# Norm factors as rows: from matrix products to a trip through device memory, with the first norm's sums taken by one column of ones

## The chip, the core and the metric

The kernel runs on one core of one Trainium2 chip. The metric is the device time of one execution in microseconds (us), as the median of several runs. TensorE is called PE below, VectorE DVE, ScalarE ACT, GpSimd POOL; SP is the engine that issues most of the DMAs, and it issues them in a fixed order.

## What is computed

One encoder layer on x (1024 positions x 1024 features, float32). Only the two norms at which the change acts are shown; attention and the delta rule lie between them.

```python
def rms_norm(x, g):
    y = x * rsqrt(mean(x * x, axis=-1) + EPS)
    return y * g

u = rms_norm(h, mix_norm_gain);  proj = u @ w_in      # 3592 columns: q, k, v, delta q, k, v, gate, decay, beta
...                                                   # band attention and gated delta rule give `mixed`
h = h + mixed
z = rms_norm(h, ffn_norm_gain) @ w_ff1                # 1024 -> 4096
h = h + square(relu(z)) @ w_ff2                       # 4096 -> 1024
```

The kernel multiplies without the norm's factor r = rsqrt(mean + EPS) of each position and applies r to the product. For the second norm the factor enters after the squared relu, as r squared, which is 1 / (mean + EPS).

## The kernel before

Activations lie transposed: features on the 128 partitions, positions along the row. A position's factor is thus needed in two forms: as a **row** (the same 512 or 1024 factors on each of the 128 partitions), to multiply a product whose positions run along the row, and as a **column** `r_col` (128 x 8, position on the partition), for products that stand the other way.

Every product of the large weights is made of three passes over high and low parts (`mm3`, line 217; `uh`/`ul` are the parts of the activations, `wdk_h`/`wdk_l` and so on those of the weights). 24 products of 128 x 128 by 128 x 512 fill one PSUM bank.

**First stage.** `load_xt` (line 232) loads the input in two halves of 512 positions (`hf` 0 and 1), splits it, and adds the squares of the features into two accumulators per half (`xs`; one is added to by DVE, the other by POOL). `first_proj` (line 354) makes the delta k projection: half 0 in four banks (three of pool `ps_a`, one of `ps_o`), half 1 in three (two of `ps_d`, one of `ps_t`). Its fourth tile is made later by `delta_proj` in a bank of `ps_a`. `row_scales` (line 304) is called once per half. It has eight products of an accumulator's 128 columns as stationary operand with one column of ones, which leave the sums as a column (`rcol`); `rsqrt` (line 184) with short instructions on DVE, one of them on POOL (`pow`), which gives `r_col`; and four products of the broadcast column with the identity, which leave the row in PSUM (`rrow`), from where ACT copies it to `rr`. `delta_proj` (line 365) then empties each bank on DVE with `raw = ps * rr` (line 378), convolves (lines 382 and 384) and writes `kT`. The same loop serves delta q (`dq`) and v (`dv`): eight tiles of 24 products each, whose banks are the three of `ps_a` in turn (`dk` half 0 tiles 0 to 2, the fourth tile of half 1, then `dq` 0, 1, 2 and so on). So `dq` tile 2 takes the bank of the fourth `dk` tile of half 1.

**Second norm, in `ff1`** (line 1259). The squares' sums over the features, gathered as `sq_dr`, come back as `acc`; `norm_col` (line 1297) makes eight column products (`hcol`) and a reciprocal on DVE (`r_col`); `norm_row` (line 1308) makes eight products with the identity (`hrow`), and ACT scales them by 1024 into `r2` (128 x 1024). `emit` (line 1355) multiplies each 128 x 1024 block `z` by `r2` on DVE (line 1356) and stores it. Blocks 0 and 1 begin before the norm is known: their first two products `z11` are held, and are multiplied by `r2` once it is there. The weights of `ff1` come by SP (line 1320), and DVE and ACT make high and low parts and sums of weights and activations for PE (lines 204, 1290, 1376, 1395).

The order of the instructions on each engine is made when the program is built: a scheduler replays the code with its own costs and sets the order on every engine, SP included. In the attention part a `Clock` with hand-made costs sets the order.

Of the kernel before, what the change touches and what calls it, by code (L numbers as in the profile page):

```python
# [98 lines left out]
def hymba_kernel(  # L99
# [53 lines left out]
    def bank(pool, name):  # L153
        return pool.tile([P, 512], F32, tag="bk", name=name)
# [29 lines left out]
    def rsqrt(st, ss, n, scale, eps, name, out=None):  # L184
        eng = nc.vector if st in RS else nc.gpsimd
        v = small(st, name + "_v", n)
        eng.tensor_scalar(v, ss, scale, eps, ALU.mult, ALU.add)
        y = small(st, name + "_y", n)
        nc.gpsimd.tensor_tensor(y, v, mhalf[:, 0:n], ALU.pow)
        t = small(st, name + "_t", n)  # L190
        r = small(st, name + "_r", n) if out is None else out
        eng.tensor_tensor(t, y, y, ALU.mult)
        if st in RS:
            nc.vector.scalar_tensor_tensor(t, t, -0.5, v, ALU.mult, ALU.mult)
            nc.vector.scalar_tensor_tensor(r, t, 1.5, y, ALU.add, ALU.mult)
            return r
        nc.gpsimd.tensor_tensor(t, t, v, ALU.mult)
        nc.gpsimd.tensor_scalar(t, t, -0.5, 1.5, ALU.mult, ALU.add)
        nc.gpsimd.tensor_tensor(r, y, t, ALU.mult)
        return r  # L200
# [96 lines left out]
    kt_dr = dram.tile([NT, P, 512], F32, name="kt_dr")  # L297
    h_dr = dram.tile([2, 2, P, 4, TH], F32, name="h_dr")
    f_dr = dram.tile([DFF // P, P, SEQ], F32, name="f_dr")
    sq_dr = dram.tile([P, SEQ], F32, name="sq_dr")  # L300

    mix = [[None, None], [None, None]]

    def row_scales(squares, hf, name, col, row):

        ps = bank(ps_t, f"{name}col{hf}")
        for q in range(TPH):
            for i, acc in enumerate(squares):
                nc.tensor.matmul(ps[:, q:q + 1], acc[:, q * P:(q + 1) * P], ones[:, 0:1], start=(i == 0),
                                 stop=(i == len(squares) - 1))  # L310
        rsqrt("a", ps[:, 0:TPH], TPH, 1.0 / DM, EPS, f"{name}{hf}", col)
        ps = bank(ps_t, f"{name}row{hf}")
        for q in range(TPH):
            nc.tensor.matmul(ps[:, q * P:(q + 1) * P], col[:, q:q + 1].broadcast_to([P, P]), ident,
                             start=True, stop=True)
        nc.scalar.copy(row, ps)

    def interleave(*gens):

# [939 lines left out]
    def ff1(R, started, psw, pools):  # L1259
# [37 lines left out]
        def norm_col():  # L1297

            acc = page2("ut4", "acc")
            nc.sync.dma_start(out=acc, in_=sq_dr)  # L1300
            ps = psw.tile([P, 1024], F32, tag="bk", name="hcol")
            nc.tensor.matmul(ps[:, 0:NT], ones, epsc, start=True, stop=False)
            for q in range(NT):
                nc.tensor.matmul(ps[:, q:q + 1], acc[:, q * P:(q + 1) * P], ones[:, 0:1], start=False, stop=q == NT - 1)
            with tc.issue_after(held[-1][2]), tc.high_priority():
                nc.vector.reciprocal(r_col, ps[:, 0:NT])

        def norm_row():

            ps = psw.tile([P, 1024], F32, tag="bk", name="hrow")  # L1310
            for q in range(NT):
                nc.tensor.matmul(ps[:, q * P:(q + 1) * P], r_col[:, q:q + 1].broadcast_to([P, P]), ident,
                                 start=True, stop=True)
            nc.scalar.mul(r2.rearrange("p a t -> p (a t)"), ps, float(DM))

        def block(sb):
            def lw(tag, name, kh, c):
# [89 lines left out]
        for i in range(2):  # L1407
            for g in first:
                next(g)
        norm_col()  # L1410
        for _ in range(2):
            next(first[0])
        norm_row()
        for emit, z, _ in held:
            emit(z, 0, 0)
        for g in first + [block(sb) for sb in range(2, DFF // FB)]:
# [259 lines left out]
```

## Time and profile before

| | |
|---|---|
| runs | 1263.95, 1261.29, 1260.56 us; median 1261.29 |
| span of the profiled execution | 1256.3 us, first to last instruction (its own device time is not recorded apart from it) |
| granted TensorE clock, mean | 0.998 |
| busy: PE / PE weight loads / DVE / ACT / POOL | 98% / 82% / 74% / 44% / 22% |
| DMA | 158.52 MB in 134374 packets, 126 GB/s on the mean |
| instructions | 17942 |

The busy time of PE is the time between the starts and modelled ends of matmuls that overlap, so 98% says that PE hardly ever stands without work. One fp32 product leaves two records on PE, one product of split (fp32r) operands leaves one. In rows of the timeline the columns are start, duration, engine, line, operation, `out<-in`, shapes and count, and in brackets the idle time before it and what ended it.

### The profile page before, as it was taken

How to read it: one execution, taken by the hardware profiler on the slowest of the kernel's cores; microseconds unless marked ns; L12 is line 12 of the kernel's file. 1: busy time of each engine (PE TensorE's matmuls, PEld its weight loads, DVE VectorE, ACT ScalarE, POOL GpSimd, SP SyncE). 2: the span in 40 equal slices, each digit the busy share in tenths (PEclk: the TensorE clock that was granted, in tenths of full speed). 3: DMA queues.
4: the chain of work that ended last, by engine and by line, in shares of the span. 5: the costliest groups of instructions: out<-in, count | busy, mean ns of one | idle time of the engine just before them, and what ended most of it. 6: DMA issues, size and time to landing. Idle time of an engine off the chain costs nothing.

```text
span 1256.3 us, 17942 instructions
## 1 busy us (share of the span) xinstructions
PE 1236.3 (98%) x6686; PEld 1032.1 (82%) x6686; DVE 932.9 (74%) x1417; ACT 548.1 (44%) x899; POOL 270.5 (22%) x458
## 2 busy tenths in 40 slices
PE   9999999999999999899999999999999999999997
PEld 8778888788889988778888788888887888888886
DVE  7899987755237568776269766767769997997988
ACT  7233132232246756655365444454444543333330
POOL 4425552253133444523200000000000000000043
PEclk9999999999999999999999999999999999999999
DMA  7214364665585633045243333333269614333002
GB/s 228 63 41 141 101 164 118 119 161 134 168 259 136 189 85 88 24 135 176 76 143 104 114 118 118 119 132 101 84 205 365 202 67 134 105 97 101 1 34 100
DMA packets 134374, 158.52 MB, mean 126 GB/s; under 512 B 31120, under 2 KB 78224, under 8 KB 133776
## 3 DMA queue, kind: packets, MB, share of 16 engines
q1 hardware_dynamic: 116192, 135.11, 35.6%
q10 hardware_dynamic: 18096, 22.29, 5.2%
q8 instruction: 52, 0.85, 0.3%
q14 instruction: 34, 0.28, 0.1%
HBM read 109.91 MB, written 47.45 MB: 125 GB/s over the span
## 4 chain that ended last, share of the span: by engine, by line
PE 55%; DVE 5%; ACT 1%; issue 1%; POOL 0%; DVEq 0%; ACTq 0%
PE p L1444 24%; PE q L1348 21%; PE op L222 7%; PE t_o L1026 1%; DVE h L1290 1%; PE t_sa L927 0%; DVE q_0a_l L204 0%; PE t_tpb L987 0%; PE t_tpa L1003 0%; PE t_sb L927 0%; PE c_pv L516 0%; ACT t_pb L966 0%; PE c_po L516 0%; PE t_tpo L520 0%; PE c_pq L516 0%
## 5 line engine op out<-in xcount | busy, mean ns | idle before, releaser
L1516 POOL TENSOR_TENSOR y<-y,y 128x1024 f32<-128x1024 f32 x4 | 11.5, 2890 | 575.7 <-DVE y L1512 570.6
L1512 DVE TENSOR_TENSOR y<-y,p 128x1024 f32<-128x1024 f32 x46 | 55.1, 1217 | 5.4 <-PE p L1444 4.5
L222 PE MATMUL op<-ml,wo_h 128*128 128x512 f32 x128 | 50.2, 395 | 0.0
L222 PE MATMUL op<-mh,wo_h 128*128 128x512 f32 x128 | 49.2, 394 | 0.8 <-ACT mh L203 0.8
L222 PE MATMUL op<-mh,wo_l 128*128 128x512 f32 x128 | 49.3, 391 | 0.0
L947 DVE CUSTOM_DVE_ANT_0 t_pb<-t_sb,biasn 128x256 f32<-128x256 f32 (+1 forms) x64 | 23.2, 401 | 31.4 <-PE t_sb L927 31.3
L966 ACT ACTIVATE t_pb<-t_pb,t_nm 128x256 f32<-128x256 f32 (+1 forms) x64 | 31.4, 491 | 17.2 <-DVE t_nm L958 15.5
L1229 DVE TENSOR_TENSOR h<-op,op_x 128x512 f32<-128x512 f32 x16 | 10.8, 686 | 29.2 <-PE op L222 29.2
L1236 POOL TENSOR_TENSOR op_q<-op_q 128x512 f32<-128x512 f32 x14 | 19.6, 1400 | 55.4 <-ACT op_q L1235 55.1
L222 PEld LDWEIGHTS op<-mh,wo_h 128*128 128x128 f32 x128 | 23.9, 188 | 6.4 <-ACT mh L203 1.2
L222 PEld LDWEIGHTS op<-ml,wo_h 128*128 128x128 f32 x128 | 24.1, 188 | 5.0 <-DVE ml L204 0.2
L222 PEld LDWEIGHTS op<-mh,wo_l 128*128 128x128 f32 x128 | 24.1, 188 | 5.0
L958 DVE CUSTOM_DVE_ANT_0 t_pa<-t_sa,biaso,t_nm 128x384 f32<-128x384 f32 (+2 forms) x48 | 24.9, 543 | 2.8 <-PE t_sa L927 1.6
L970 ACT ACTIVATE t_pa<-t_pa,t_nm 128x384 f32<-128x384 f32 (+2 forms) x48 | 26.5, 552 | 0.0
L222 PE MATMUL aq_ps<-waq_h,ul 128*128 128x512 f32 x64 | 25.5, 399 | 0.0
L222 PE MATMUL dq_ps<-uh,wdq_h 128*128 128x512 f32 x64 | 25.5, 399 | 0.0
L222 PE MATMUL dv_ps<-ul,wdv_h 128*128 128x512 f32 x64 | 25.5, 399 | 0.0
L222 PE MATMUL dq_ps<-ul,wdq_h 128*128 128x512 f32 x64 | 25.3, 396 | 0.0
L222 PE MATMUL g_ps<-ul,wg_h 128*128 128x512 f32 x64 | 25.2, 394 | 0.0
L927 PE MATMUL t_sb<-ks,t_q 128*128 128x256 f32 (+1 forms) x144 | 24.0, 294 | 1.3 <-DVE t_nm L947 1.3
L222 PE MATMUL g_ps<-uh,wg_h 128*128 128x512 f32 x64 | 25.2, 394 | 0.0
L222 PE MATMUL aq_ps<-waq_h,uh 128*128 128x512 f32 x64 | 25.2, 396 | 0.0
(1109 smaller groups left out, 4304.3 us busy)
## 6 DMA issues: line engine op xcount, KB each, us to landing
wa<-in_w_ff_dram SPq DMA_DIRECT2D x32, 512.0 KB, 4.0
a<-in_w_ff_dram SPq DMA_DIRECT2D x32, 512.0 KB, 3.8
b<-f_dr SPq DMA_DIRECT2D x32, 512.0 KB, 3.4
f_dr<-yy ACTq DMA_DIRECT2D x16, 512.0 KB
t_q<-q_dr SPq DMA_DIRECT2D x30, 256.0 KB, 3.6
f_dr<-zz ACTq DMA_DIRECT2D x13, 512.0 KB
ks<-k_dr SPq DMA_DIRECT2D x16, 256.0 KB, 7.8
wo_r<-in_w_out_dram SPq DMA_DIRECT2D x16, 256.0 KB, 5.2
```

Of the source, the lines that this page charges most:

```text
L222: nc.tensor.matmul(ps, a, b, start=(first and i == 0), stop=(last and i == n - 1))
L927: nc.tensor.matmul(o, q[m][:, i * P:(i + 1) * P], k[:, c], start=(m == 0), stop=(m == 1))
L947: nc.vector.tensor_tensor_reduce(sb[:, c], bk[:, c], new[g][pp][:, c], -1.0, 3.0e38, ALU.add, ALU.min, nm[:, 4 + i:5 + i])
L958: nc.vector.tensor_tensor_reduce(sa[e][:, 0:wa], bk[:, 0:wa], old[g][i][:, 384 - wa:384], -1.0, nm[:, 4 + i:5 + i], ALU.add, ALU.min, nm[: ...
L966: nc.scalar.activation(sb[:, c], sb[:, c], AF.Exp, bias=m, scale=-1.0, accum_out=T["sums"][:, 4 + i:5 + i])
L970: nc.scalar.activation(sa[e][:, 0:wa], sa[e][:, 0:wa], AF.Exp, bias=m, scale=-1.0, accum_out=T["sums"][:, i:i + 1])
L1026: return nc.tensor.matmul(po[64 * e:64 * e + 64, pp * P:(pp + 1) * P], vt[k0 + j][:, 64 * h:64 * h + 64], (ta[e] if j < na else tb)[:, c:c ...
L1236: nc.gpsimd.tensor_tensor(acc, acc, sq, ALU.add)
L1290: nc.vector.tensor_tensor(t, wide(R[a], i), wide(R[b], i), ALU.subtract)
L1348: nc.tensor.matmul(part(ps, q), l[:, s], r, start=(k + m == 0), stop=(k == 3 and m == 2))
L1444: nc.tensor.matmul(part(ps[q], 0) if by_rows else part(ps[q // 2], q % 2), l[:, s], part(r, k), start=(i + k + m == 0), stop=(i + k + m == 4))
L1512: nc.vector.tensor_tensor(y[i][m], y[i][m], ps[m], op)
```

## The change

`row_scales` now first adds the second accumulator into the first on POOL, and multiplies once per half with **one column of ones as the stationary operand** and the 512 columns of the accumulator moving: one fp32 product of 1 x 512 in place of eight. ACT copies the row of sums to partition 0 of a page (`line`, `rss`), and four DMAs on SP follow: the sums to memory (`ss_dr`), back as a column of 128 x 4 (single 4-byte elements), after `rsqrt` the column of factors to memory (`rr_dr`, again 4-byte elements), and from there as a row to all 128 partitions (`rr`, 256 KB). `norm_row` loses its eight products and the ACT step: the column `r_col`, now scaled by 1024 by one more DVE instruction, goes to memory (`rf_dr`, 1024 elements of 4 bytes) and comes back on 128 partitions (`r2`, 512 KB), both on SP; it is called right after `norm_col`, before two further steps of block 0.

```diff
+    ss_dr = dram.tile([2, TH], F32, name="ss_dr")
+    rr_dr = dram.tile([2, TH], F32, name="rr_dr")
+    rf_dr = dram.tile([NT, P], F32, name="rf_dr")
...
+        a0, a1 = squares
+        nc.gpsimd.tensor_tensor(a0, a0, a1, ALU.add)
         ps = bank(ps_t, f"{name}col{hf}")
-        for q in range(TPH):
-            for i, acc in enumerate(squares):
-                nc.tensor.matmul(ps[:, q:q + 1], acc[:, q * P:(q + 1) * P], ones[:, 0:1], start=(i == 0),
-                                 stop=(i == len(squares) - 1))
-        rsqrt("a", ps[:, 0:TPH], TPH, 1.0 / DM, EPS, f"{name}{hf}", col)
-        ps = bank(ps_t, f"{name}row{hf}")
-        for q in range(TPH):
-            nc.tensor.matmul(ps[:, q * P:(q + 1) * P], col[:, q:q + 1].broadcast_to([P, P]), ident,
-                             start=True, stop=True)
-        nc.scalar.copy(row, ps)
+        nc.tensor.matmul(ps[0:1, :], ones[:, 0:1], a0, start=True, stop=True)
+        line = page("pp", f"{name}ss{hf}")[0:1, :]
+        nc.scalar.copy(line, ps[0:1, :])
+        nc.sync.dma_start(out=ss_dr[hf:hf + 1], in_=line)
+        ss = small("a", f"{name}ss{hf}", TPH)
+        nc.sync.dma_start(out=ss, in_=ss_dr[hf].rearrange("(q p) -> p q", p=P))
+        rsqrt("a", ss, TPH, 1.0 / DM, EPS, f"{name}{hf}", col)
+        nc.sync.dma_start(out=rr_dr[hf].rearrange("(q p) -> p q", p=P), in_=col)
+        nc.sync.dma_start(out=row, in_=rr_dr[hf:hf + 1].rearrange("a t -> (a t)").partition_broadcast(P))
...
                 nc.vector.reciprocal(r_col, ps[:, 0:NT])
+                nc.vector.tensor_scalar(r_col, r_col, float(DM), None, ALU.mult)
         def norm_row():
-            ps = psw.tile([P, 1024], F32, tag="bk", name="hrow")
-            for q in range(NT):
-                nc.tensor.matmul(ps[:, q * P:(q + 1) * P], r_col[:, q:q + 1].broadcast_to([P, P]), ident,
-                                 start=True, stop=True)
-            nc.scalar.mul(r2.rearrange("p a t -> p (a t)"), ps, float(DM))
+            nc.sync.dma_start(out=rf_dr.rearrange("q p -> p q"), in_=r_col)
+            nc.sync.dma_start(out=r2.rearrange("p a t -> p (a t)"),
+                              in_=rf_dr.rearrange("q p -> (q p)").partition_broadcast(P))
...
         norm_col()
+        norm_row()
         for _ in range(2):
             next(first[0])
-        norm_row()
```

The scheduler sets the engines' order anew, and it differs from before in the first quarter of the program and around the second norm. SP in the first stage, before (the loads of the weights of delta q and delta v stand in one piece; `xt` is the input of half 1):

```order
L239 DMA xt_485<-in_x_t_dram 128x512
L210 DMA wdq_r<-in_w_in_dram 128x512 x8
L210 DMA wdv_r<-in_w_in_dram 128x512 x5
L560 DMA kt_dr<-d_kt 128x512
L352 DMA dq_dr<-dq_y 128x4x128 x2
```

and now:

```order
L239 DMA xt_483<-in_x_t_dram 128x512
L210 DMA wdq_r<-in_w_in_dram 128x512 x5
L315 DMA ss_dr<-rss_426 1x512
L317 DMA rss_429<-ss_dr 128x4x1
L319 DMA rr_dr<-r_col 128x4x1
L320 DMA rr_422<-rr_dr 128x512
L315 DMA ss_dr<-rss_568 1x512
L317 DMA rss_571<-ss_dr 128x4x1
L210 DMA wdq_r<-in_w_in_dram 128x512 x3
L210 DMA wdv_r<-in_w_in_dram 128x512 x3
L319 DMA rr_dr<-r_col 128x4x1
L320 DMA rr_564<-rr_dr 128x512
```

Six of the eight new DMAs stand between the fifth and the sixth load of delta q's weights, the last two among delta v's.

DVE at half 1's factors (`dk_raw` empties a bank with the row `rr`, `kT` ends a tile), before:

```order
L394 SCALAR_TENSOR_TENSOR kT_600<-dk_th,dk_y 128x128 x4
L378 TENSOR_TENSOR dk_raw<-dk_ps,rr_566 128x512 x2
L204 TENSOR_TENSOR wdv_l<-wdv_r,wdv_h 128x512
L382 TENSOR_SCALAR dk_y<-dk_raw,cw 128x512
L384 SCALAR_TENSOR_TENSOR dk_y<-dk_raw,cw,dk_y 128x512 x3
```

and now:

```order
L204 TENSOR_TENSOR wdv_l<-wdv_r,wdv_h 128x512
L388 SCALAR_TENSOR_TENSOR dk_y<-dk_raw,cw,dk_y 128x512 x2
L382 TENSOR_TENSOR dk_raw<-dk_ps,rr_564 128x512 x2
L386 TENSOR_SCALAR dk_y<-dk_raw,cw 128x512
L398 SCALAR_TENSOR_TENSOR kT_593<-dk_th,dk_y 128x128 x4
```

The last tile of half 0 is now ended after the first two banks of half 1 are emptied, where it was ended ahead of them.

DVE at the second norm (`r` is the row `r2`, `z` the held blocks, the others parts and sums for PE), before:

```order
L1306 RECIPROCAL r_col<-hcol 128x8
L204 TENSOR_TENSOR q_0a_l<-wa_0_7326,q_0a_h 128x1024
L1290 TENSOR_TENSOR h_6842<-h_6626,h_6842 128x1024 x2
L204 TENSOR_TENSOR q_0a_l<-wa_0_7489,q_0a_h 128x1024
L204 TENSOR_TENSOR t3l_7643<-h_7128,t3h_7642 128x1024
L204 TENSOR_TENSOR t3l_7648<-h_7128,t3h_7647 128x1024
L1384 TENSOR_TENSOR yy_7328<-yy_7328,q_0_7536 128x1024
L1376 TENSOR_TENSOR ws_1_7729<-wa_1_7725,wa_1_7727 128x1024
L204 TENSOR_TENSOR q_0a_l<-wa_0_7491,q_0a_h 128x1024
L1356 TENSOR_TENSOR z_0_7439<-z_0_7439,r_7323 128x1024
```

and now:

```order
L1310 RECIPROCAL r_col<-hcol 128x8
L204 TENSOR_TENSOR q_0a_l<-wa_0_7319,q_0a_h 128x1024
L1294 TENSOR_TENSOR h_6835<-h_6619,h_6835 128x1024 x2
L204 TENSOR_TENSOR q_0a_l<-wa_0_7485,q_0a_h 128x1024
L1311 TENSOR_SCALAR r_col<-r_col 128x8
L204 TENSOR_TENSOR t3l_7629<-h_7121,t3h_7628 128x1024
L204 TENSOR_TENSOR t3l_7634<-h_7121,t3h_7633 128x1024
L1387 TENSOR_TENSOR yy_7321<-yy_7321,q_0_7532 128x1024
L1379 TENSOR_TENSOR ws_1_7715<-wa_1_7711,wa_1_7713 128x1024
L204 TENSOR_TENSOR q_0a_l<-wa_0_7487,q_0a_h 128x1024
L1388 TENSOR_TENSOR yy_7321<-yy_7321 128x1024
L1359 TENSOR_TENSOR z_0_7432<-z_0_7432,r_7316 128x1024
```

The scaling by 1024 stands four wide instructions behind the reciprocal, and one more wide instruction stands ahead of the first use of the row.

## The prediction

> **What bounds the kernel now.** I read the page's busy slices first, then the busy time by stretches at the two places that change, then the timelines there.
>
> From the page, the span in 40 slices:
>
> ```profile
> PE   9999999999999999899999999999999999999997
> DVE  7899987755237568776269766767769997997988
> ```
>
> Busy time by stretches (columns: stretch and its length in us, then busy us and instructions of PE, PE weight loads, DVE, ACT, POOL; granted clock; DMA share; GB/s):
>
> ```profile
> 30.00:40.00 10.00, 10.00 (x53) 8.53 (x54) 6.73 (x9) 3.19 (x7) 5.93 (x4) 1.00 0.20 53
> 40.00:100.00 60.00, 60.00 (x292) 46.94 (x291) 57.60 (x123) 18.57 (x35) 19.73 (x36) 1.00 0.19 57
> 640.00:690.00 50.00, 49.91 (x237) 41.65 (x236) 49.08 (x45) 32.61 (x35) 0.00 (x0) 1.00 0.30 99
> ```
>
> PE is never idle at either place, at the full clock, so a product taken away there is time. But DVE has 57.60 of 60 and 49.08 of 50 us too: it follows close behind, and what makes DVE later takes the gain back. A factor's row is what DVE starts with.
>
> **PE work, first norm.** Timeline of PE at half 1's sums and at its row:
>
> ```profile
> 48.20 1.84 PE L309 MATMUL rcol<-ones,xs 128*128 128x1 f32 x16
> 49.90 0.48 PE L222 MATMUL dk_ps<-uh,wdk_h 128*128 128x512 f32 x1
> 50.22 0.39 PE L222 MATMUL dk_ps<-ul,wdk_h 128*128 128x512 f32 x1
> 50.45 0.39 PE L222 MATMUL dk_ps<-uh,wdk_l 128*128 128x512 f32 x1
> ...
> 59.16 1.05 PE L314 MATMUL rrow<-ident,r_col 128*128 128x128 f32 x8
> 59.97 0.48 PE L222 MATMUL dq_ps<-uh,wdq_h 128*128 128x512 f32 x1
> 60.28 0.40 PE L222 MATMUL dq_ps<-ul,wdq_h 128*128 128x512 f32 x1
> ```
>
> Starts count here, since matmuls overlap. Large products start 0.23 us apart (50.22 to 50.45). The sums take 49.90 - 48.20 = 1.70, and the product behind them 0.32 for 0.23, so 1.79 per half; the row takes 0.81 + 0.09 = 0.90. For two halves 5.4 us go. Two fp32 products of 512 columns come. None so wide stands in the trace. Two records at the 0.23 of a 512-column record make 0.46; four times an fp32 product of 128 columns (0.81 / 4 = 0.20) make 0.81. I take 0.81 + 0.09, the row of the same number type; two halves 1.8. So PE is 3.6 us ahead (4.3 by the lower bound).
>
> **The way of the row, half 0.** Before:
>
> ```profile
> 36.10 0.15 DVE L187 TENSOR_SCALAR r_v<-rcol 128x4 f32<-128x4 f32 x1
> ...
> 37.78 0.16 DVE L195 SCALAR_TENSOR_TENSOR r_col<-r_t,r_y 128x4 f32<-128x4 f32 x1
> 40.09 1.29 DVE L378 TENSOR_TENSOR dk_raw<-dk_ps,rr 128x512 f32<-128x512 f32 x2 [2.15 <-ACT rr L316]
> ```
>
> ```profile
> 31.52 1.15 ACT L250 ACTIVATE xt<-xt 128x512 f32<-128x512 f32 x2
> 39.48 0.59 ACT L316 COPY rr<-rrow 128x512 f32<-128x512 f32 x1 [6.81 <-PE rrow L314]
> ```
>
> ```profile
> 34.50 0.33 SPq L210 DMA_DIRECT2D wdq_r<-in_w_in_dram  x1
> ```
>
> DVE begins to empty banks at 40.09. Now ACT copies the row of sums when its squares are done (31.52 + 1.15 = 32.7), for about the 0.59 that a copy of 512 columns takes: 33.3. On SP it stands behind the fifth load of delta q's weights, issued at 34.50, which waits for a weight split on DVE; that split now stands ahead of three additions of squares, so SP is free between 33.1 and 34.8. I take 33.5. Four DMAs follow, each waiting for the one before or for `rsqrt`. The nearest landing times, from the DMA issues (last number: median us from issue to landing):
>
> ```profile
> a_dr<-d_A SPq DMA_DIRECT2D x8, 256.0 KB, 2.0
> op_x<-in_x_t_dram SPq DMA_DIRECT2D x16, 256.0 KB, 2.6
> dtb<-in_dn_dt_bias_dram SPq DMA_DIRECT2D x1, 2.0 KB, 2.5
> acc<-sq_dr SPq DMA_DIRECT2D x1, 512.0 KB, 3.8
> ```
>
> A store lands in 2.0, a load of 256 KB in 2.6, a small one in 2.5 (beside other traffic; bounds 2.0 and 3.0). `rsqrt` takes 37.94 - 36.10 = 1.84. So 33.5 + 2.0 + 2.2 + 1.8 + 2.0 + 2.6 = 44.1, and about 0.1 for each of four hand-overs: 44.5. DVE starts **4.4 us late**. The bounds: every hop 0.3 shorter and SP free at 33.1, 2.8 late; hops of 3.0, 3.0, 3.0 and 3.5 and SP free at 34.8, 9 late. Below zero it can't go: from 33.3 to 40.09 there are 6.8 us, and four landings at the shortest of these rows, 2.0, are 8.
>
> What hides it: PE works on half 1 until 48.2, in banks that need no row. Its next bank, for the fourth tile of half 1, is wanted at about 47 and is free at 44.5 + 0.7. Behind that DVE has no pause in which to catch up. The first bank where it counts is that of `dq` tile 2, which needs the fourth `dk` tile of half 1 emptied:
>
> ```profile
> 62.66 1.29 DVE L378 TENSOR_TENSOR dk_raw<-dk_ps,rr 128x512 f32<-128x512 f32 x2 [0.56 <-ACT rr L316]
> ...
> 71.98 0.68 DVE L378 TENSOR_TENSOR dk_raw<-dk_ps,rr 128x512 f32<-128x512 f32 x1
> ```
>
> ```profile
> 75.95 0.39 PE L222 MATMUL dq_ps<-uh,wdq_h 128*128 128x512 f32 x1
> ```
>
> It was free at 71.98 + 0.68 = 72.66 and PE came at 75.95, **3.3 us of slack**. Now PE could come at 72.4, and the bank is free at 72.7 + 4.4 less a pause of half a us ahead of 62.66 that goes: 76.6. PE waits 4.2 us and is 0.6 behind its old time. In general PE ends this stage (DVE's delay - 0.5 - 3.3) late, but never more than 3.6 (4.3) early: -1.0 at the short hops, +5 at the long ones.
>
> **Half 1.** Its sums are copied behind the first `tanh` on ACT, at about 50; with the same hops and DVE's queue between, its factors are stored at about 60 and its row lands at about 64.8. DVE, 4.4 late, wants it at 64 to 66.5. No further term, but no margin either: where hops are longer, this row is late by the same sum. The six DMAs that stand ahead of delta q's last three weight loads hold SP until about 52; those loads were issued from 53.06 on before, since they wait for splits:
>
> ```profile
> 53.06 0.88 SPq L210 DMA_DIRECT2D wdq_r<-in_w_in_dram  x2
> ```
>
> Nothing is lost there.
>
> **POOL and the small terms.** An addition of 512 columns on POOL, and the first column product of half 0:
>
> ```profile
> 28.39 1.47 POOL L251 TENSOR_TENSOR xs<-xs,xt 128x512 f32<-128x512 f32 x1 [5.80 <-ACT xt L250]
> ```
>
> ```profile
> 25.36 0.28 PE L309 MATMUL rcol<-ones,xs 128*128 128x1 f32 x2
> ```
>
> The squares of half 0 are ready before 25.36, and its added sum 1.5 later, ahead of PE's product at about 30; half 1's stands where DVE waits for the row. Both cost nothing.
>
> **Second norm.** Rows of PE, ACT and DVE:
>
> ```profile
> 667.48 1.95 PE L1312 MATMUL hrow<-ident,r_col 128*128 128x128 f32 x16
> ```
>
> ```profile
> 669.46 1.03 ACT L1314 ACTIVATE r<-hrow 128x1024 f32<-128x1024 f32 x1 [0.96 <-PE hrow L1312]
> ```
>
> ```profile
> 667.57 1.22 DVE L204 TENSOR_TENSOR q_0a_l<-wa,q_0a_h 128x1024 fp32r<-128x1024 f32 x1
> ...
> 673.24 1.22 DVE L204 TENSOR_TENSOR q_0a_l<-wa,q_0a_h 128x1024 fp32r<-128x1024 f32 x1
> 674.38 2.36 DVE L1356 TENSOR_TENSOR z<-z,r 128x1024 f32<-128x1024 f32 x2
> ```
>
> and the chain that ended last, a little later:
>
> ```profile
> 688.08 1.15 DVE q_1a_l L204
> 689.23 0.04 issue
> 689.27 7.57 PE q L1348 x32
> ```
>
> About 1.8 us of PE go. But at 689.27 PE starts a product as soon as DVE has ended the operand, and DVE is busy for 49.08 of the 50 us up to 690: PE now comes earlier and waits. That gain is nothing. DVE gets one short instruction (0.2). The row: the scaling stands behind the instruction of 667.57, so at 668.8; issue at 669.0, a store of 2.0 to 3.0, a load of 512 KB like `acc` with 3.8: 675.0 to 676.0. DVE wants it at 674.4 + 1.1 (one wide instruction moved ahead) + 0.2 = 675.7. So 0 to 0.3 of waiting, each us more goes to the end. I take +0.4 in all, bounds 0 and +3.
>
> **The sum.** 1256.3 + 0.6 + 0.4 = 1257.3 us of span; the median of the runs is 5.0 us above this span, which the change doesn't touch: 1261.3 + 1.0 = **1262.3 us**. The attention part between is ordered as before, so it moves as a whole. 0.3% is 3.8 us, about what a measurement can tell from no change.
>
> **Rivals.** (1) *The lead is kept.* If the hops are near the short bound, or DVE finds pauses among the weight splits, PE keeps 1 to 3.6 us, and with half 1's row early and the second norm's 1.8 us too: 1256 to 1258. For it: PE is the engine that is always busy. Against: four landings in line against 3.3 us of slack. (2) *Stores of single elements are slow.* Half 0's column of factors is 512 elements of 4 bytes, the second norm's 1024. What the trace shows is only a load: 1024 pieces of 32 bytes (`wab`) in this stretch of 1.8 us.
>
> ```profile
> DMA packets 1298, 0.05 MB, mean 25 GB/s; under 512 B 1298, under 2 KB 1298, under 8 KB 1298
> ```
>
> A small store to memory doesn't stand in it. If a store of single elements lands in 4 us and the two other small transfers in 3, DVE starts 4.4 + 2.0 + 1.0 + 0.8 = 8.2 late: PE +4.4; the second norm's row comes at 669.0 + 4.0 + 3.8 + 0.2 = 677.0: +1.3, and 0.2 for the scaling. Together 1267.2. It decides once DVE starts 7 us late. The Trainium skill, "DMA: Bandwidth & Descriptors", Specifications, says that a transfer below 512 bytes is a read-modify-write, and its Rules for kernel authors that a strided last dimension makes one descriptor per element; by these the change pays here, but they give no time, and no run here shows it yet. (3) *Half 1's row is the late one* while half 0's is in time: +1 to +2 more, 1263 to 1264.5.
>
> **Chances.** Forecast 0.50, all within 0.3%; (1) 0.17, of it 0.12 faster by over 0.3%, 0.05 within; (2) 0.25, 0.24 of it slower; (3) 0.08, within but for 0.01. So faster 0.12, same 0.63, slower 0.25. The range runs from the lead kept in part (1258.0) to the slow stores (1268.0).
>
> **What would show it.** PE: no column products, two of 512 columns of 0.8 to 0.9 us each; a wait of about 4 us at `dq` tile 2 or just before (the first transposes of `kT`), and one of 1 to 2 at 689 of before. DVE: idle before the first use of `rr`, which starts at 44 to 45; no idle above 1 us before the first use of `r2`. SP: the two element stores landing within 2 to 2.5 us. Wrong is the forecast if DVE starts before 42 or after 47.5, if PE doesn't wait after 70, or if time goes in the attention part, where nothing should change.

## The result, and the profile after

The changed kernel takes **1295.22 us** (median of four runs, 1289.53 to 1297.00), the kernel before beside it 1261.05 us. The ratio is 1.0261, with a 95% interval of 1.0237 to 1.0286: 34.2 us slower. The forecast was 1262.3 us, with a range up to 1268.

In its profiled execution (span 1293.5 us) SP's timeline shows the new DMAs. The columns are start, duration of the issue, engine, line, `out<-in`:

```profile
32.82 0.30 SPq L315 DMA_DIRECT2D ss_dr<-rss  x1
35.15 0.40 SPq L317 DMA_DIRECT2D rss<-ss_dr  x1
41.33 0.37 SPq L319 DMA_DIRECT2D rr_dr<-r_col  x1
49.37 0.34 SPq L320 DMA_DIRECT2D rr<-rr_dr  x1
59.29 0.24 SPq L315 DMA_DIRECT2D ss_dr<-rss  x1
60.44 0.37 SPq L317 DMA_DIRECT2D rss<-ss_dr  x1
...
71.41 0.38 SPq L319 DMA_DIRECT2D rr_dr<-r_col  x1
79.21 0.33 SPq L320 DMA_DIRECT2D rr<-rr_dr  x1
```

```profile
694.88 0.37 SPq L1315 DMA_DIRECT2D rf_dr<-r_col  x1
705.50 0.34 SPq L1316 DMA_DIRECT2D r<-rf_dr  x1
```

Each load waits for the store before it. So the store of half 0's 512 single elements landed in 49.37 - 41.33 = **8.04 us**, half 1's in 7.80, and the second norm's 1024 in **10.62**. The store of the sums as one line took 35.15 - 32.82 = 2.33. On DVE:

```profile
37.38 0.16 DVE L187 TENSOR_SCALAR r_v<-rss 128x4 f32<-128x4 f32 x1
38.68 1.24 DVE L192 TENSOR_TENSOR r_t<-r_y 128x4 f32<-128x4 f32 x1 [1.14 <-POOL r_y L189]
...
40.16 1.15 DVE L195 SCALAR_TENSOR_TENSOR r_col<-r_t,r_y 128x4 f32<-128x4 f32 x1
54.09 1.29 DVE L382 TENSOR_TENSOR dk_raw<-dk_ps,rr 128x512 f32<-128x512 f32 x2 [12.79 <-DMA rr<-rr_dr]
```

```profile
84.20 1.29 DVE L382 TENSOR_TENSOR dk_raw<-dk_ps,rr 128x512 f32<-128x512 f32 x2 [8.25 <-DMA rr<-rr_dr]
```

```profile
709.48 2.36 DVE L1359 TENSOR_TENSOR z<-z,r 128x1024 f32<-128x1024 f32 x2 [7.82 <-DMA r<-rf_dr]
```

DVE starts half 0 at 54.09 instead of 40.09 (14.0 late), half 1 at 84.20 instead of 62.66 (21.5 late), and stands 7.82 us in front of the second norm's blocks. PE stands behind DVE; its waits are in the brackets of its timeline:

```profile
54.83 0.79 PE L222 MATMUL dk_ps<-uh,wdk_h 128*128 128x512 f32 x1 [7.31 <-DVE dk_raw L382]
...
55.85 0.63 PE L222 MATMUL dk_ps<-uh,wdk_l 128*128 128x512 f32 x1
56.28 0.63 PE L222 MATMUL dk_ps<-uh,wdk_h 128*128 128x512 f32 x1
```

```profile
84.95 0.90 PE L524 MATMUL d_tp<-ident,kT 128*128 128x128 f32 x3 [7.25 <-DVE dk_raw L382]
94.34 0.50 PE L222 MATMUL dq_ps<-uh,wdq_h 128*128 128x512 f32 x1 [2.48 <-DVE dk_raw L382]
```

```profile
714.16 0.79 PE L1351 MATMUL q<-t1h,q_1a_l 128*128 128x512 f32 x1 [9.02 <-DVE q_1a_l L204]
```

Those four waits are 26.1 us. The two products after the first wait show a second loss: they start 0.43 us apart (55.85 to 56.28) where the same product took 0.23. Busy time by stretches says why, in the column behind POOL's (the granted clock, 0.50 there):

```profile
40.00:100.00 60.00, 42.09 (x165) 28.94 (x164) 38.38 (x84) 12.68 (x25) 16.15 (x24) 0.86 0.20 45
52.00:56.00 4.00, 1.17 (x3) 0.97 (x4) 1.88 (x4) 0.00 (x0) 0.57 (x2) 0.50 0.29 62
84.00:88.00 4.00, 2.76 (x8) 2.07 (x9) 3.76 (x9) 0.00 (x0) 0.00 (x0) 0.50 0.20 73
```

From 40 to 100 PE has work for 42.09 of 60 us, where it had 60.00 before. Counting each run of large products that start 0.36 to 0.5 us apart, and what goes beyond 0.23, the slow clock costs about 8 us in this execution: 3.5 between 50 and 100, 2.4 behind 714, 0.8 behind 254 and 1.4 behind 993.

The rest of the time between is not as before either. The first and the last product of the attention's own projections (`ak_ps`, `av_ps`), before and then now:

```profile
211.59 0.39 PE L222 MATMUL ak_ps<-wak_h,uh 128*128 128x512 f32 x1
359.90 0.39 PE L222 MATMUL av_ps<-wav_h,ul 128*128 128x512 f32 x1
```

```profile
231.79 0.39 PE L222 MATMUL ak_ps<-wak_h,uh 128*128 128x512 f32 x1
384.99 0.39 PE L222 MATMUL av_ps<-wav_h,ul 128*128 128x512 f32 x1
```

So 20.2 us are lost before the attention part, **4.9 more in its projections** (148.3 us long before, 153.2 now), about 1 from there to the second norm, and 11.3 from the second norm on. In these projections the instructions of PE, DVE and ACT stand in another order than before. PE's wait for DVE at `ak_tp` is 3.66 us instead of 1.88 there, and the slow clock costs 0.8; what makes the rest is not shown. Part of it can be chance: in `second_pieces` below, whose order there is that of before, the same stretch takes 149.8.

Before's profiled execution was a quick one (its span lies 5.0 us under the median of its runs, after's 1.7 under), so some 3 of the 37.2 us between the spans are not the change's, and below the times of whole kernels are compared by the medians of their runs.

### The profile page after: what moved, and what is told of

It reads as the page before. It is cut to its first block, busy times and chain, and to the rows that moved or that the text cites. A ratio compares the mean times of both kernels' runs of the same rounds, so it can differ in the third digit from the quotient of the medians.

```text
span 1293.5 us, 17841 instructions
## 1 busy us (share of the span) xinstructions
PE 1244.1 (96%) x6626; PEld 1031.4 (80%) x6626; DVE 936.9 (72%) x1418; ACT 546.5 (42%) x898; POOL 269.9 (21%) x460
## 4 chain that ended last, share of the span: by engine, by line
PE 54%; DVE 4%; DMA 2%; ACT 1%; issue 1%; POOL 0%; SPq 0%; DVEq 0%
PE p L1447 23%; PE q L1351 21%; PE op L222 6%; PE t_o L1030 1%; DMA rf_dr<-r_col 1%; DMA wo_r<-in_w_out_dram 1%; DVE h L1294 1%; PE t_sa L931 0%; PE t_tpb L991 0%; DMA r<-rf_dr 0%; DVE q_0a_l L204 0%; PE t_sb L931 0%; PE c_pv L520 0%; PE t_tpa L1007 0%; PE t_tpo L524 0%
## 5 line engine op out<-in xcount | busy, mean ns | idle before, releaser
L222 PE MATMUL dq_ps<-uh,wdq_l 128*128 128x512 f32 x64 | 26.3, 411 | 0.0
L222 PE MATMUL ak_ps<-wak_h,uh 128*128 128x512 f32 x64 | 25.5, 404 | 0.2 <-ACT wak_h L203 0.2
L222 PE MATMUL ak_ps<-wak_l,uh 128*128 128x512 f32 x64 | 25.7, 403 | 0.0
L222 PE MATMUL ak_ps<-wak_h,ul 128*128 128x512 f32 x64 | 25.4, 400 | 0.0
L395 ACT ACTIVATE dk_th<-dk_y 128x512 f32<-128x512 f32 x8 | 5.1, 632 | 48.1 <-DVE dk_y L388 46.7
```

The lines of the kernel that those rows point to most:

```text
L222: nc.tensor.matmul(ps, a, b, start=(first and i == 0), stop=(last and i == n - 1))
```

## The experiments

**The two places apart.** Against the changed kernel, `first_old` (first diff) has the old `row_scales`, `second_old` (second diff) the old `norm_row`, called where it stood, without the scaling on DVE:

```diff
-        nc.gpsimd.tensor_tensor(a0, a0, a1, ALU.add)
...
-        nc.sync.dma_start(out=row, in_=rr_dr[hf:hf + 1].rearrange("a t -> (a t)").partition_broadcast(P))
+        for q in range(TPH):
+            for i, acc in enumerate(squares):
...
+        nc.scalar.copy(row, ps)
```

```diff
-            nc.sync.dma_start(out=rf_dr.rearrange("q p -> p q"), in_=r_col)
...
+            for q in range(NT):
+                nc.tensor.matmul(ps[:, q * P:(q + 1) * P], r_col[:, q:q + 1].broadcast_to([P, P]), ident,
+                                 start=True, stop=True)
+            nc.scalar.mul(r2.rearrange("p a t -> p (a t)"), ps, float(DM))
```

> The first norm as before the change, the second norm through memory as in the changed kernel. Theory A: 11 to 12 us over before, 1272 to 1274, all of it from 690 of before on (PE's wait of 9.0 us there, and its lower clock behind it). If the two places act on each other, the sum of this run's and the next one's difference is not the 34 us of the whole change, but off by more than 3.

> The first norm's factors through memory, the second norm as before the change. Theory A: 22 to 25 us over before, 1283 to 1286, with DVE starting at 54 and at 84 as in the changed kernel. If the places don't act on each other, this and the run before add up to the 34 us of the whole change within 3.

Measured: `first_old` 1270.74 us against 1260.76, ratio 1.0076 (1.0059 to 1.0093), 10.0 us, a little under what was expected; `second_old` 1283.54, ratio 1.0183 (1.0168 to 1.0198), 22.8 us. Together 32.8 of 34.2: the two places add up. In `first_old` DVE stands in front of `z` as in the changed kernel:

```profile
684.69 2.36 DVE L1358 TENSOR_TENSOR z<-z,r 128x1024 f32<-128x1024 f32 x2 [7.37 <-DMA r<-rf_dr]
```

**Single elements or the trip.** `pieces` stores what a partition holds side by side; the row then holds the factors in another order.

```diff
-        nc.sync.dma_start(out=rr_dr[hf].rearrange("(q p) -> p q", p=P), in_=col)
+        nc.sync.dma_start(out=rr_dr[hf].rearrange("(p q) -> p q", p=P), in_=col)
...
-            nc.sync.dma_start(out=rf_dr.rearrange("q p -> p q"), in_=r_col)
+            nc.sync.dma_start(out=rf_dr, in_=r_col)
```

> The changed kernel, but each partition's factors are stored side by side: 128 pieces of 16 bytes (first norm) and of 32 bytes (second norm) in place of 512 and 1024 single elements. The factors then stand in another order in the row, so the output is not the layer's; the number and the sizes of all instructions are the same. Theory A (single elements): the two stores land in 2.0 to 3.5 us instead of 8.0 and 10.6; DVE starts at 48 to 49.5 instead of 54.1, the second norm's z waits 0 to 1 us instead of 7.8, and the kernel takes 1264 to 1275. Theory B (the trip itself, stored and read back at once): stores land as late as before, 1292 to 1298. Theory C (the clock that PE gets after a wait is most of the loss): the waits shrink as by A but the time stays over 1280.

Measured: 1274.18 us, ratio 1.0108 (1.0093 to 1.0123). About 21 of the 34 us are gone with two access patterns; the instructions are the same in number and size. That decides for theory A as far as these 21 us go. SP's timeline of `pieces`:

```profile
41.75 0.33 SPq L319 DMA_DIRECT2D rr_dr<-r_col  x1
43.30 0.32 SPq L320 DMA_DIRECT2D rr<-rr_dr  x1
```

The store lands in 1.55 us. But 13 us stay.

**What is slow in the store.** Three kernels make DMAs alone, each waiting for the one before. The form of all is a store from SBUF to memory, a load of what was stored, and a DVE step on what was loaded, from which the next store takes its source:

```python
sync.dma_start(out=view(d), in_=src)      # the store under test
sync.dma_start(out=back, in_=d[0:1, 0:1])  # is issued when the store has landed
nc.vector.tensor_scalar(src[0:1, 0:1], back[0:1, 0:1], 1.0, None, ALU.mult)
```

(The first kernel loads up to four elements back, or the whole row.)

> The layer is left out here: this kernel makes nothing but DMAs, one after the other on SP with nothing else in flight, each waiting for the one before, and its output is filled with constants. Theory A (single elements): the landing of a store grows with the number of 4-byte elements in it. From the two sizes seen in the changed kernel (512 elements 8.0 us, 1024 elements 10.6 us) the line is 5.4 us + 5.1 ns per element: 6.0 for 128, 6.7 for 256, 15.8 for 2048. Pieces of 16 bytes and more, and one line of 2 KB, land in 2.0 to 3.0. If what costs is that neighbouring elements are written into the same short stretch of memory, 512 elements that lie 512 bytes or 2 KB apart land in 2 to 4 us; if it is the count of pieces alone, they take 8 too. Theory B (the trip): whatever is stored and then read back at once lands late, 5 to 8 us for lines and pieces as well. Row load: if the fresh store makes it slow, the second load of the same row takes 2.6 and the first 4.7; if it is that 128 partitions read the same 2 KB, both take 4.7, a row of the weights' input does so too, and a load of 128 different rows takes 2.6.

SP's timeline of the first, for 512 neighbouring elements (`s_e`) and for 512 elements that lie 64 bytes apart (`s_gap`); a store's landing is the start of the next row less its own:

```profile
13.25 0.38 SPq L90 DMA_DIRECT2D s_e<-c  x1
21.06 0.33 SPq L94 DMA_DIRECT2D b_s_e<-s_e  x1
...
74.96 0.36 SPq L90 DMA_DIRECT2D s_gap<-c  x1
76.82 0.23 SPq L94 DMA_DIRECT2D b_s_gap<-s_gap  x1
```

7.81 us side by side, 1.86 with gaps of 64 bytes or of 2 KB, for the same number of elements. The DMA view of the first store, from its issue to its landing:

```profile
DMA  0000075000000000000000000000000000000000
DMA packets 528, 0.00 MB, mean 0 GB/s; under 512 B 528, under 2 KB 528, under 8 KB 528
```

All packets are over a fifth of the way in; then the DMA engines stand idle for 6 us, and the store still hasn't landed. Who looks only at packets and their durations sees nothing slow. The line of theory A through two sizes fell: 128 elements took 6.5, 256 took 7.85 and 2048 11.0, where it gave 6.0, 6.7 and 15.8. Theory B fell too: a line and pieces land in 1.2 to 2.9. The first kernel also put too many loads into the queue at once to price a row load; the second does that.

> As the first kernel of DMAs alone: the layer is left out, and each DMA waits for the one before. In that kernel 512 elements landed in 7.8 us when they lay side by side and in 1.9 to 2.1 when 64 bytes or more lay between them, with the same packets. Theory A, now narrower: writes into the same 64 bytes wait for each other, about 0.4 us each, and different stretches of 64 bytes don't. Then a store of n neighbouring elements takes 1.2 us + 0.4 us x (n - 1) up to n = 16, and no more beyond: 1 element 1.2, 2 1.6, 4 2.4 to 2.9, 8 4.0 to 4.5, 16 6.5 to 7.5, 32 and 64 and 128 the same 6.5 to 8. 512 elements 8 bytes apart (8 in 64 bytes) 4.0 to 4.7, 16 bytes apart (4) 2.4 to 3.0, 32 bytes apart (2) 1.6 to 2.2, 128 apart 1.9. Rival A2: it is the stretch of 512 bytes (or of more) in which writes wait for each other; then the time grows up to 128 neighbouring elements, 16 elements land in under 2.5 us, and 128 bytes apart (4 in 512) still costs more than 64 bytes did in the first kernel. The queue is not the cause: from ACT's queue 512 neighbouring elements land in 7 to 8.5 as well. Row loads of 256 KB: behind an element store 4.5 to 5.2, behind a store of one line or of 16-byte pieces and for rows of the input 3.3 to 3.8, 128 different rows 2.6 to 3.0; if the element store itself delays the read, the second load of the same row takes 3.3 to 3.8.

> DMAs alone again, the layer is left out. The landings so far (neighbouring elements: 16 1.35 us, 32 3.21, 64 6.51, 128 7.24, 512 7.9; 512 elements 8 bytes apart 4.16, 16 apart 2.69, 32 apart 1.89, 64 apart 1.79) contradict both theories of the run before: 16 elements in one stretch of 64 bytes are quick, and nothing grows beyond 64 elements. Theory F: writes into the same 256 bytes wait for each other, about 0.1 us each, and different stretches of 256 bytes don't. Then two groups of 32 land in 6 to 7 us if they lie in the same 256 bytes (128 bytes apart) and in 3 to 3.6 if 256 or 512 bytes apart; four groups of 16 in 6 to 7 if 64 bytes apart, in 3 to 3.6 if 128 apart (two groups in each stretch), in 1.3 to 1.8 if 256 bytes or 2 KB apart; two or eight groups of 64, 256 bytes or 2 KB apart, in 6.5 to 8. Rival G: it is the number of elements up to 64, wherever they lie within some KB; then all groups of 64 elements in all land in 6 to 7, at any distance. Rival H: stretches of 128 bytes; then two groups of 32 land in 3.2 at 128 bytes apart already.

Landings in us, each from two rows of SP's timeline as above:

| store | landing |
|---|---|
| 1, 4, 8 neighbouring elements | 1.14, 1.17, 1.18 |
| 16, 32, 48, 64, 96 | 1.35, 3.20, 5.45, 6.52, 6.07 |
| 128 (three stores) | 6.52, 7.03, 7.29 |
| 256, 512, 1024, 2048 | 7.85, 7.81, 8.24, 11.04 |
| 512 elements 8, 16, 32, 64, 128 bytes apart | 4.17, 2.68, 1.89, 1.84, 1.98 |
| 128 pieces of 16, 32, 64 bytes | 2.90 and 1.45 (two stores), 1.42, 1.46 |
| one line of 2 KB; 128 lines of 2 KB | 1.18; 2.01 |

By the expectations of the second kernel both theories fell. 16 elements within 64 bytes are quick, which speaks against 64 bytes; nothing grows from 64 to 512 elements, which speaks against 512 and more. The third kernel (`m4_stretch`) sets `g` groups of `k` neighbours at a pitch, the destination being `d[:, 0:k].rearrange("g k -> k g")` of a `[g, pitch]` tile. 64 elements in two groups of 32:

```profile
12.67 0.33 SPq L93 DMA_DIRECT2D s_32x_by128b<-big  x1
18.18 0.23 SPq L87 DMA_DIRECT2D land<-s_32x_by128b  x1
20.97 0.30 SPq L93 DMA_DIRECT2D s_32x_by256b<-big  x1
23.90 0.23 SPq L87 DMA_DIRECT2D land<-s_32x_by256b  x1
```

5.51 us when both groups lie in the same 256 bytes, 2.93 when they don't. Four groups of 16: 5.88 at 64 bytes apart, 2.46 at 128, 1.37 at 256 bytes, 1.38 at 2 KB. Rival G would have all of these at 6 to 7, and rival H the first pair at 3.2; both fell. That is theory F, its numbers a little below the forecast at 128 bytes: the times are as if **writes into the same 256 bytes waited for each other, some 0.1 us each beyond the first 16**. What does it inside the chip no run shows, and it is not the whole law. Beyond 64 neighbours the time hardly grows. Eight groups of 64 land in 8.01 when 256 bytes apart but in 12.80 when 2 KB apart, and the same 512 neighbouring elements, which took 7.8 to 8.9 in five stores (8.01 from ACT's queue), took 10.66 in one; 1024 took 8.24 here and 10.62 in the layer. Part of the wait shows only in the load behind the store: one element comes back in 1.2 to 1.4 us behind 1 to 8 neighbours, in 2.65 behind 16, whose store itself lands in 1.35. All that stays open.

The Trainium skill, "DMA: Bandwidth & Descriptors", Specifications, has a transfer under 512 bytes as a read-modify-write. Here pieces of 4 bytes with 64 bytes between them, and of 32 bytes, land in 1.4 to 1.9 us: being small alone costs next to nothing, being crowded does.

Row loads by the second kernel, from the DMA's issue to DVE's step: 2.6 to 2.8 for 128 different rows, 3.1 to 3.5 for one row to all 128 partitions, 4.0 for that right behind a store of single elements, and 3.15 for a later load of such a row. So the broadcast costs about 0.5, and the store before it delays the read as well.

**The clock.** In `m3_clock` DVE works alone between runs of 60 products (`gap` is `n` instructions of DVE that make the next operand `t`):

```python
for i, n in enumerate((0, 1, 3, 5, 8, 11, 14, 20)):
    t = gap(i, n, t)
    run(60, "r", t)
```

> The layer is left out: PE makes 60 products of 128 x 128 by 128 x 512 at a time, 13.7 us at 0.23 us each, and DVE alone works in the pauses between, which grow from about 1 to 15 us. Theory C (PE's clock falls behind a wait): after pauses of 7 us and more the granted clock is about 0.5 for some 4 us, products start 0.45 us apart there, and a run of 60 takes 2 to 4 us longer; after pauses of 1 us nothing is lost; somewhere between is the pause from which it costs. If the lower clock in the changed kernel came from something else than the pause, all runs of 60 take the same time.

```profile
52.10 13.90 PE L84 MATMUL bank<-m 128*128 128x512 f32 x60 [3.42 <-DVE m L91]
70.88 15.50 PE L84 MATMUL bank<-m 128*128 128x512 f32 x60 [4.87 <-DVE m L91]
93.43 16.13 PE L84 MATMUL bank<-m 128*128 128x512 f32 x60 [7.05 <-DVE m L91]
```

Pauses of 1.2, 2.0 and 3.4 us cost nothing beyond themselves (13.89, 13.89, 13.90); those of 4.9, 7.1, 9.2, 11.4 and 15.8 us cost 1.4 to 2.2 us more, whatever their length. So a long pause alone lowers the clock, as theory C has it, at a smaller price than "2 to 4". The Trainium skill, "TensorE: Matmul & The Clock Gate", What's actually happening, has the clock halved behind an idle window of about 3.4 us; these pauses agree. In the changed layer three waits are over 7 us, with 0.8 to 2.4 us of slow products behind each.

In the layer, though, shorter waits are often followed by slow products too. Behind the wait of 2.48 us at 94.34 they cost 1.5 us. Behind a wait of 1.8 us at `p50b` in `ff2` they cost 1.4 to 1.6 in eight profiled executions and nothing in two (before and `half1`). So no limit on the length of a wait can be read from these runs; that the waits from 4.9 us on all cost something can.

**What is left without single elements.** `layout` has the positions in their right order and no element store: a partition gets four neighbouring positions (eight in the second norm, by column products that take every eighth column), and `r_col` is loaded afterwards. `layout_early` also takes half 1's trip off the work behind half 0's row.

```diff
+        nc.sync.dma_start(out=ss, in_=ss_dr[hf].rearrange("(p q) -> p q", p=P))
+        c4 = rsqrt("a", ss, TPH, 1.0 / DM, EPS, f"{name}{hf}")
+        nc.sync.dma_start(out=rr_dr[hf].rearrange("(p q) -> p q", p=P), in_=c4)
...
+        nc.sync.dma_start(out=col, in_=rr_dr[hf].rearrange("(q p) -> p q", p=P))
...
+                nc.tensor.matmul(ps[:, q:q + 1], acc.rearrange("k (p q) -> k p q", q=NT)[:, :, q], ones[:, 0:1], start=False,
+                                 stop=q == NT - 1)
```

and in `layout_early` besides, for half 1 (`copied` holds the copies of the sums):

```diff
+        c4 = rsqrt("a", ss, TPH, 1.0 / DM, EPS, f"{name}{hf}", None, bool(hf))
...
+                    with tc.issue_after(copied[-1]) if not hf and not ct else ExitStack():
+                        nc.scalar.activation(th, y, AF.Tanh)
```

> The whole layer, with the factors' round trip in the same order of positions but without stores of single elements: the sums come back as 128 pieces of 16 bytes (four neighbouring positions on a partition), the factors are stored the same way, the row is loaded, and the column r_col is loaded after it from the same memory (a load of single elements, not in a hurry). In the second norm the column products take every eighth position, so that each partition's eight factors are neighbours. Theory A: as the pieces run, 1270 to 1276. Theory B (the trip of four DMAs costs the rest, with half 1's trip starting only after half 0's row has come): it does not come below 1268, DVE starts at 46 to 48 and half 1's row is there at 70 to 75.

> As the run before, and half 1's trip is taken off the work that waits for half 0's row: the copy of its sums stands ahead of the first tanh on ACT, and its rsqrt is made on POOL alone. If the rest of the loss in the first stage is that the two trips stand in line (theory B), half 1's sums are copied by 48 instead of 52, its row lands by 60 to 66 instead of 74, DVE's wait for it and PE's wait at the transposes of kT go, and the kernel takes 1263 to 1268. If the rest is half 0's lateness alone (7 us against 3.3 us of slack), nothing changes: 1270 to 1276.

Measured: `layout` 1273.84 us, ratio 1.0101 (1.0086 to 1.0116); `layout_early` 1273.56, 1.0100 (1.0084 to 1.0116). First use of the two rows in `layout`, then in `layout_early`:

```profile
46.72 1.29 DVE L383 TENSOR_TENSOR dk_raw<-dk_ps,rr 128x512 f32<-128x512 f32 x2 [5.61 <-PE dk_ps L367]
...
73.19 1.29 DVE L383 TENSOR_TENSOR dk_raw<-dk_ps,rr 128x512 f32<-128x512 f32 x2 [2.65 <-DMA rr<-rr_dr]
```

```profile
47.57 1.29 DVE L384 TENSOR_TENSOR dk_raw<-dk_ps,rr 128x512 f32<-128x512 f32 x2 [5.69 <-DMA rr<-rr_dr]
...
68.69 0.69 DVE L384 TENSOR_TENSOR dk_raw<-dk_ps,rr 128x512 f32<-128x512 f32 x1 [2.67 <-DMA rr<-rr_dr]
```

In the first row the named releaser, PE, had long been done; it is the row's DMA. Theory B fell in its simple form: half 1's row was used 4.5 us sooner and the time stayed. The trace of `layout_early` does reach the attention part 1.9 us sooner (first `ak_ps` product at 217.98 instead of 219.85), but 1.35 of that are gone at the end of the attention's projections. The edit moved it less far than meant (68.69, not 60 to 66), and DVE's order, made anew, asked for the row sooner, so that the wait for it is the same 2.7 us. The share of each half was measured alone, with the other half and the second norm by products (`half0` has the first of these lines, `half1` the second):

```diff
+        if hf != 0:
...
+        if hf != 1:
...
+            nc.scalar.copy(row, ps)
+            return
```

> Only half 0 of the first norm goes through memory, with stores in pieces as in the layout run; half 1's factors and the second norm are made by products as before. Theory D (half 0's lateness alone makes the loss that is left): DVE starts at 46 to 48 as in the layout run, 6.5 late, and the kernel takes 1268 to 1274, as with both halves. Theory E (each half's trip costs its own share): DVE starts as late, but the time is 1263 to 1267. By the prediction's own rule for such a delay (delay - 0.5 - 3.3 us, here 2.8) and without a cost of the clock it would be 1263 to 1264.

> Only half 1 goes through memory, with stores in pieces; half 0 and the second norm are made by products as before. Theory D: DVE starts at 40 to 41 as before, half 1's row lands at 62 to 66, and the kernel takes 1260 to 1263. Theory E: half 1's row is late here too, DVE waits for it 3 us or more, and the kernel takes 1264 to 1268.

Measured: `half0` 1264.80 us, ratio 1.0033 (1.0021 to 1.0044), 4.0 us; `half1` 1264.89, 1.0029 (1.0016 to 1.0042), about 4 us. In `half0` DVE starts at 46.24, in `half1` half 1's row makes it wait 2.67 us at 69.13. Both times are in theory E's ranges, though half 1's wait is a little under its "3 us or more": each trip has its own price, also when the other one is not there. But only part of that price falls in the first stage. The first `ak_ps` product starts at 214.44 in `half0` and 214.16 in `half1`, against 212.0 to 212.1 in the two kernels with the old first norm (`first_old` and `second_pieces`): 2.1 to 2.5 us each. The scheduler's order of the attention's projections is another one in both kernels, and in `half0` they take 152.7 us, against 148.3 to 149.8 with before's order. What the trip costs and what the new order costs has not been measured apart.

`second_pieces` has the old `row_scales` and `layout`'s second norm:

```diff
-            nc.sync.dma_start(out=rf_dr.rearrange("q p -> p q"), in_=r_col)
+            nc.sync.dma_start(out=rf_dr, in_=r_col)
```

> The first norm is as before the change; the second norm's factors go through memory, but each partition's eight factors are neighbours, so that the store has 128 pieces of 32 bytes. If the store of 1024 single elements was all that cost in the second norm, the store lands in 1.4 to 2.0 us, the row is there before DVE wants it, and the kernel takes 1260 to 1262: no gain either, since DVE sets the pace there. If something else of the change costs there (the additional step on DVE, SP's weight loads held behind the trip), it takes over 1264.

Measured: 1262.94 us, ratio 1.0021 (1.0010 to 1.0033). SP and DVE:

```profile
670.63 0.34 SPq L1315 DMA_DIRECT2D rf_dr<-r_col  x1
672.11 0.34 SPq L1316 DMA_DIRECT2D r<-rf_dr  x1
```

```profile
677.51 2.36 DVE L1359 TENSOR_TENSOR z<-z,r 128x1024 f32<-128x1024 f32 x2
```

The store lands in 1.48, and DVE has no idle time before `z`. So the 10.0 us of the second norm were the store, but for about 2: the time lies between the two expectations. A place for these 2 us stands in the traces. The column products now take every eighth column as stationary operand; before, and then in `second_pieces`:

```profile
660.19 1.84 PE L1304 MATMUL hcol<-ones,acc 128*128 128x1 f32 x16
```

```profile
661.92 3.74 PE L1307 MATMUL hcol<-ones,acc 128*128 128x1 f32 x16
```

They last 1.9 us longer, as in both `layout` kernels, about what the products of the row had cost, and large products start 0.43 us apart behind them (1.5 us lost from 667 to 670). `pieces`, without that view, has neither at this place. That this is all of the 2 us is not shown. In any case the change in PE's products brings nothing there. 4.0 + 4 + 2.1 make about 10 of `layout`'s 12.9; the intervals (each about 1.5 us either way) leave room for the rest, or for some interplay of the two halves.

**The products alone.** `sums4` is the kernel before with POOL's addition of the two accumulators, so that four column products stand where eight stood.

```diff
+        nc.gpsimd.tensor_tensor(a0, a0, a1, ALU.add)
...
-            for i, acc in enumerate(squares):
-                nc.tensor.matmul(ps[:, q:q + 1], acc[:, q * P:(q + 1) * P], ones[:, 0:1], start=(i == 0),
-                                 stop=(i == len(squares) - 1))
+            nc.tensor.matmul(ps[:, q:q + 1], a0[:, q * P:(q + 1) * P], ones[:, 0:1], start=True, stop=True)
```

> The kernel before with one part of the change alone: POOL adds the two accumulators, so that four column products are made per half instead of eight; rows are still made by products, and the second norm is as before. If a product taken from PE in the first stage is time (the prediction's term), PE is 1.8 us ahead for two halves, and the kernel takes 1258.5 to 1260. If DVE follows too close behind (rival), or POOL's addition delays the factors, it takes 1260 to 1262.

Measured: 1264.06 us (12 runs), ratio 1.0029 (1.0016 to 1.0042), slower than both expected. PE waits 1.7 us at `rrow` for `r_col`, a wait that before did not have, and DVE starts at 40.80 instead of 40.09. `r_col` lasts 1.11 us instead of 0.16 and ends with POOL's addition for half 1 beside it. So the products that PE is spared in half 0 come back as a wait. But that is not the 3 us: the first `ak_ps` product starts at 212.50, 0.4 to 0.5 later than in `first_old` and `second_pieces`, and the attention's projections, in another order again, take 150.6 us (148.3 before). So this kernel doesn't measure the addition alone, and most of its loss lies behind the first stage. No version tried here beats the kernel before.

## Why the prediction was wrong, point by point

- **PE's terms held.** The product of 1 x 512 (`rcol`) starts at 29.55 and the next product at 30.50, 0.95 for the 0.90 forecast:

```profile
29.55 1.02 PE L312 MATMUL rcol<-xs,ones 128*1 128x512 f32 x2
30.50 0.50 PE L366 MATMUL dk_ps<-uh,wdk_h 128*128 128x512 f32 x1
```

- **The step that failed is the landing of the element stores**, taken at 2.0 us from `a_dr` (rows of 2 KB). Half 0's way, forecast and measured: SP free 33.5, 32.82; store of the line 2.0, 2.33; load 2.2, 2.23; `rsqrt` 1.8, 3.95; element store 2.0, **8.04**; row load 2.6, **4.72**. The measured hops end at 54.09, where DVE starts. Rival (2) named the right step and priced it at 4 us per store, half or less of what it is; with 8.0 and 10.6 in its own formula (12.2 late, so 8.4 for PE; 7.9 and 0.2 at the second norm) it would have said 1278, still 17 us short. A bound taken "from the nearest rows" was no bound: no row of before showed many small writes side by side.
- **`rsqrt`** took 2.1 us more. `r_t` and `r_col` last 1.24 and 1.15 us instead of 0.16, and each ends when an addition of POOL beside it ends (38.61 + 1.29 = 39.90, 39.98 + 1.29 = 41.27):

```profile
38.61 1.29 POOL L251 TENSOR_TENSOR xs<-xs,xt 128x512 f32<-128x512 f32 x1
39.98 1.29 POOL L310 TENSOR_TENSOR xs<-xs,xs 128x512 f32<-128x512 f32 x1
```

  The second of them is the addition that the change brought, and that the prediction put at nothing.
- **Row load.** 2.6 was the price of 128 different rows. A broadcast is 3.1 to 3.5, and 4.0 right behind an element store; the rest of the 4.7 stays open.
- **Half 1: "no further term" was wrong.** Its sums stand behind the first `tanh` on ACT, as the prediction had it, but that `tanh` now waits for half 0's row:

```profile
58.17 0.63 ACT L395 ACTIVATE dk_th<-dk_y 128x512 f32<-128x512 f32 x1 [24.33 <-DVE dk_y L388]
58.71 0.56 ACT L314 COPY rss<-rcol 1x512 f32<-1x512 f32 x1
```

  So the two trips stand in line, with 12.8 and 8.25 us of waiting on DVE. The prediction did say that there was no margin if hops are longer.
- **The rule "PE ends late by the delay - 0.5 - 3.3"** gives 10.2 for 14.0, and 20.2 were lost before the attention part; it has no second wait and no clock. Where only half 0 is late (`half0`, 6.2 late), it gives 2.4, and the trace is 2.3 to 2.5 later than the kernels with the old first norm when the attention begins: there the rule holds. The rest of the 4.0 measured (2.6 to 5.5) came behind it.
- **"The attention part between is ordered as before, so it moves as a whole" was wrong.** The order of its projections is another one, and they take 4.9 us more in the changed kernel's trace (0 to 1.4 more in the two kernels that keep before's order). The prediction had named time lost there as a sign of being wrong. What of it the order causes is not shown.
- **A term that was missing is the clock.** Each of the waits over 7 us costs PE another 0.8 to 2.4 us, and some shorter ones about 1.5.
- **Second norm.** The load was right (3.98 for 3.8), the store was 10.62 instead of 2.0 to 3.0. That PE's gain is worth nothing there was right.
- **The base.** "5.0 us above this span, which the change doesn't touch" took one execution for the rule; the spans of eight of the ten other kernels lie 1.0 to 2.1 under the median of theirs. The forecast is an offset from the median, so the time is not changed by it.

## What to carry to other kernels

Before a small transpose goes through memory, look at how many pieces of its store fall into the same 256 bytes: 512 elements of 4 bytes side by side landed in 7.8 us, the same 2 KB as 16-byte pieces in 1.5 to 2.9 and as one line in 1.2. Give each partition neighbouring elements, so that the order is made by the load, where single elements cost no such wait (512 of them came back in 2.2 us); but if products then have to take every eighth column for it, look at their price as well (3.7 us instead of 1.8 here). Price a wait of PE not only by its length: from 4.9 us on the clock took 0.8 to 2.6 us more each time, and behind shorter waits often about 1.5. And where a scheduler sets the order anew, a kernel "with one part changed" differs in other places too: compare the traces stage by stage before a difference is put down to that part.

## What had not been expected of the hardware

- A store's packets can all be over 1.3 us after its issue, and the store lands 6.5 us later; the landing shows only in the next instruction that waits for it.
- That time goes by crowding (groups within 256 bytes of each other), not by count: 512 elements land in 7.81 us side by side and in 1.86 with 64 bytes from one to the next.
- A load right behind such a store is slow too: a single element came back in 2.85 us behind 512 neighbouring elements, in 1.2 to 1.4 behind elements 64 or 128 bytes apart.
- Short DVE instructions (0.16 us) lasted 1.1 to 1.2 us beside an addition on POOL, and ended with it.
- 16 records of one-column products with every eighth column as stationary operand lasted 3.74 us instead of 1.84.
